# Attention steps and state-space links ahead of fill products in a list scheduler, with paired whole-float32 score products and norm sums as small products

## The chip, the cores and the metric

One core of a Trainium2 chip runs the whole program. The metric is the device time of one execution in microseconds; the kernel before was timed three times (2448.54, 2445.88 and 2444.16 us, median 2445.88). One more execution was profiled; all rows below are from it.

## The reference

The input is one sequence of 512 tokens with 1024 features. Four blocks follow each other, all in float32, each a mixer and a SwiGLU feed-forward layer, with RMS norms ahead of each:

1. a bidirectional mLSTM mixer;
2. a windowed attention: 16 query heads, 4 key heads of 64 features, blocks of 128 queries that see the block before, their own and the next one, with a learned sink;
3. a parallel mixer: an attention that keeps 128 keys per query by an index score (8 index heads of 64, top-k), next to a Mamba-2 state-space part (16 heads, chunks of 128). Ahead of it stand the final norm of the first network and the norm of the second one;
4. a short convolution mixer.

```python
# index score and selection (parallel mixer)
il = jnp.einsum('bthd,bsd->bths', iq_blk, ik) * (IDX_DIM ** -0.5)
score = jnp.einsum('bths,bth->bts', jax.nn.relu(il), iw_blk)
_, sel = lax.top_k(score, topk)
...
# both attentions
p = softmax(q @ k.T * 64 ** -0.5 + mask);  o = p @ v
...
# state-space part, per chunk
y_diag = jnp.einsum('bclsgr,bcsgrp->bclgrp', cb[..., None] * decay, xdt)
hs = hs * dec[..., None, None] + st
```

## The kernel before

The activations stay in eight tiles `xT` (128 features x 512 tokens). A weight product takes three float32r products: weight and activation are each split in a high and a low part (`whi`, `wlo`; `xh`, `xl`), and `mm3` or `mm3n` (L205 to L214) adds high x high, high x low and low x high in a PSUM bank. ScalarE makes the high part (L171) and VectorE or GpSimd the low one (L166).

The program is written once, in Python, and a list scheduler then sets the order on each engine: an instruction's place in the program is its priority, and among those whose inputs are there, by the scheduler's own clock, the earliest in the program goes first. So the order of the text decides who goes first, and PSUM banks (eight, dealt out by `share` to the tags g, s, t and o) and buffers decide when something can start.

**Norm** (`norm`, L255 to L311). Squares are summed over the eight tiles on VectorE (L272), `col_sums` (L236) makes column sums by products with ones (L239), `rsqrt_cols` (L226) runs three Newton steps on 128x4 values, and `bcast_rows` (L242) spreads the result by four transposes (L245). Ahead of the parallel mixer there are two norms one after the other: each tile is squared, scaled in place by the final norm's weight (L277), split (L279, L280) and squared again, and the second factor is worked out from the first (L291 to L298).

**Window attention** (`window`, L947). `attend(g, c, y)` (L1003) does four heads of one query block: two pairs of score products with 64 contracted rows (L1015; the two heads of a pair stand on partitions 0 to 63 and 64 to 127), mask and maximum on VectorE (L1020), exponential on ScalarE (L1023), transposes (L1027), a copy (L1030, L1032), products with the values into two halves of a bank (L1036), and a last scaling by transposed reciprocals (L1047, L1050). Between the 16 calls stand fill products: the remaining query projections with `rope`, and parts of the output product. Banks are 1, 3, 3, 1 for g, s, t, o.

**Parallel mixer** (`parallel`, L1077). `index` (L1144) makes index scores, per head with a stacked high/low query (`pair_stack`, L926) and key (`key_stack`, L932): one product over 128 rows (L943) and one over 64 (L944). `topk_rounds` (L1169) finds the 128 largest per row in 16 rounds of MAX8 and MATCH_REPLACE8 on VectorE for each of three query blocks; `pump` issues some of them between other work. `att_head` (L1374) is one head of one block: three float32r score products (L1380), mask (L1381), exponential (L1387), transposes (L1391), a split of the probabilities in high and low (L1393 on ScalarE, L1394 on VectorE) and three products with split values (L1402). `fill` issues projections for the state-space part (24 products each) between the heads. Then `group_start`, `group_block` and `group_end` (L1465, L1522, L1547) make the chunk states (transposes L1470 and L1483, state products L1492, scaling L1485 to L1497), the outputs (L1531, L1534, decays from a DMA in `decays`) and a norm, with the output product `add_out` (L323) between them.

## Time and profile before

| | |
|---|---|
| runs (median of 3) | 2445.88 us |
| profiled execution, its own time | 2444.67 us |
| its span, first to last instruction | 2442.9 us |
| around the span | 1.8 us |
| TensorE (PE) busy | 2387.8 us, 98% of the span |
| weight loads (PEld) | 2055.9 us, 84% |
| VectorE (DVE) | 1804.2 us, 74% |
| ScalarE (ACT) | 1198.3 us, 49% |
| GpSimd (POOL) | 361.2 us, 15% |
| DMA | 93 GB/s on average |
| chain of work that ended last | PE 90%, DVE 5%, DMA 2% |
| granted TensorE clock, mean | 0.99 |

An instruction's busy time on PE has a modelled end and overlaps the next one; how much PE time a product takes is therefore read from one start to the next, and the chain of waits prints just that. A whole-float32 product is recorded as two MATMULs, a float32r product as one, so "x4" of a score line in the chain is two score products. Window attention runs from about 604 to 830 us, the double norm from 1160, index scores from 1211, top-k and attention of the parallel mixer to 1411, and the state-space part to about 1530 us.

### The profile page before, as it was taken

Reading aid. Unit: us, or ns where it says so; the run is one execution under the profiler, and the core shown is the slowest. Engines: PE = TensorE matmul, PEld = TensorE weight load, DVE = VectorE, ACT = ScalarE, POOL = GpSimd, SP = SyncE. Lnnn points to the kernel's source line nnn. Section 1 sums busy time; section 2 is a strip of 40 time slices with the busy share of each in tenths; the row PEclk is TensorE's granted clock in tenths of the full one; section 3 lists DMA queues with packets and bytes.
Section 4 is the critical chain, followed back from the end, with each engine's and each line's share of the span. In section 5 each row is a group of like instructions: output and inputs, shape, how many; then the busy total and the mean of one; then the engine's idle time right before and its main releaser. Section 6 shows DMA issues by size and latency. Waiting matters only on the chain.

```text
span 2442.9 us, 36706 instructions
## 1 busy us (share of the span) xinstructions
PE 2387.8 (98%) x13956; PEld 2055.9 (84%) x13956; DVE 1804.2 (74%) x3063; ACT 1198.3 (49%) x2226; POOL 361.2 (15%) x252
## 2 busy tenths in 40 slices
PE   8999999999999999999899989999999999999998
PEld 7898899998656899999677867888989788899997
DVE  7676798777564787877789778786867755668877
ACT  4444545454464554545566564553635324445444
POOL 2210001010320001010354145100100010000100
PEclk9999999999999999999999999999999999999999
DMA  5332232323211232323222132232323323223232
GB/s 167 117 100 61 78 117 96 113 87 119 82 51 35 69 113 88 120 87 110 78 71 61 53 111 87 87 100 82 121 87 104 104 96 100 81 88 120 87 104 78
DMA packets 73440, 226.64 MB, mean 93 GB/s; under 512 B 10336, under 2 KB 14576, under 8 KB 73264
## 3 DMA queue, kind: packets, MB, share of 16 engines
q1 hardware_dynamic: 68896, 220.00, 28.0%
q10 hardware_dynamic: 4320, 4.21, 0.6%
q8 instruction: 109, 1.79, 0.3%
q14 instruction: 67, 0.55, 0.1%
q0 software_dynamic: 48, 0.10, 0.0%
HBM read 219.45 MB, written 2.20 MB: 91 GB/s over the span
## 4 chain that ended last, share of the span: by engine, by line
PE 90%; DVE 5%; DMA 2%; ACT 1%; issue 1%; POOL 0%; ACTq 0%; SPq 0%; POOLq 0%; DVEq 0%
PE ps_g L206 7%; PE ps_g L208 7%; PE ps_g L207 7%; PE ps_s L206 4%; PE ps_s L208 4%; PE ps_s L207 4%; PE ps_g L446 4%; PE ps_g L444 4%; PE ps_g L445 4%; PE ps_t L206 3%; PE ps_t L207 3%; PE ps_t L208 3%; PE ps_t L446 3%; PE ps_t L445 3%; PE ps_t L444 3%; PE ps_s L1015 2%
## 5 line engine op out<-in xcount | busy, mean ns | idle before, releaser
L171 ACT ACTIVATE whi<-wraw 128x512 fp32r<-128x512 f32 (+1 forms) x726 | 447.3, 621 | 667.7 <-PE ps_g L207 236.6
L166 DVE TENSOR_TENSOR wlo<-wraw,whi 128x512 fp32r<-128x512 f32 x666 | 490.3, 746 | 188.5 <-ACT whi L171 176.1
L206 PE MATMUL ps_g<-xh,whi 128*128 128x512 f32 (+1 forms) x696 | 279.7, 404 | 2.9 <-DVE ct L1611 2.1
L424 POOL TENSOR_TENSOR S<-wraw 128x1024 f32<-128x1024 f32 x36 | 106.9, 2971 | 1173.3 <-DMA wraw<-in_in_dram 760.3
L207 PE MATMUL ps_g<-xl,whi 128*128 128x512 f32 (+1 forms) x696 | 278.1, 400 | 0.0
L208 PE MATMUL ps_g<-xh,wlo 128*128 128x512 f32 (+1 forms) x696 | 277.8, 399 | 0.0
L171 ACT ACTIVATE whi<-S 128x512 fp32r<-128x512 f32 x288 | 178.2, 628 | 191.3 <-PE ps_g L445 58.2
L166 DVE TENSOR_TENSOR wlo<-S,whi 128x512 fp32r<-128x512 f32 x288 | 199.8, 719 | 34.8 <-ACT whi L171 32.9
L444 PE MATMUL ps_g<-thi,whi 128*128 128x256 f32 x576 | 164.1, 285 | 2.7 <-ACT whi L171 1.9
L446 PE MATMUL ps_g<-thi,wlo 128*128 128x256 f32 x576 | 164.1, 285 | 0.2
L206 PEld LDWEIGHTS ps_g<-xh,whi 128*128 128x128 f32 (+1 forms) x696 | 132.1, 190 | 37.8 <-issue 5.6
L445 PE MATMUL ps_g<-tlo,whi 128*128 128x256 f32 x576 | 163.7, 284 | 0.0
L208 PEld LDWEIGHTS ps_g<-xh,wlo 128*128 128x128 f32 (+1 forms) x696 | 132.0, 190 | 31.6 <-issue 4.4
L207 PEld LDWEIGHTS ps_g<-xl,whi 128*128 128x128 f32 (+1 forms) x696 | 132.2, 190 | 29.1 <-issue 3.5
L444 PEld LDWEIGHTS ps_g<-thi,whi 128*128 128x128 f32 x576 | 111.4, 193 | 3.3 <-ACT whi L171 2.1
L446 PEld LDWEIGHTS ps_g<-thi,wlo 128*128 128x128 f32 x576 | 111.4, 193 | 0.7 <-DVE wlo L166 0.7
L445 PEld LDWEIGHTS ps_g<-tlo,whi 128*128 128x128 f32 x576 | 111.3, 193 | 0.0
L166 POOL TENSOR_TENSOR wlo<-wraw,whi 128x512 fp32r<-128x512 f32 (+1 forms) x60 | 81.0, 1359 | 153.4 <-ACT whi L171 110.5
L207 PE MATMUL ps_s<-hlo,whi 128*128 128x512 f32 x264 | 102.8, 389 | 0.0
L208 PE MATMUL ps_s<-hhi,wlo 128*128 128x512 f32 x264 | 102.7, 389 | 0.0
L206 PE MATMUL ps_t<-hhi,whi 128*128 128x512 f32 x264 | 102.7, 389 | 0.0
L207 PE MATMUL ps_t<-hlo,whi 128*128 128x512 f32 x264 | 102.7, 389 | 0.0
(545 smaller groups left out, 6641.2 us busy)
## 6 DMA issues: line engine op xcount, KB each, us to landing
wraw<-in_in_dram SPq DMA_DIRECT2D x176, 512.0 KB, 3.5
wraw<-in_down_dram SPq DMA_DIRECT2D x82, 512.0 KB, 3.6
wraw<-in_par_in_dram SPq DMA_DIRECT2D x30, 512.0 KB, 3.3
wraw<-in_mlstm_in_dram SPq DMA_DIRECT2D x24, 512.0 KB, 3.6
wraw<-in_sc_in_dram SPq DMA_DIRECT2D x24, 512.0 KB, 3.5
wraw<-in_attn_in_dram SPq DMA_DIRECT2D x12, 512.0 KB, 3.4
wraw<-in_par_out_dram SPq DMA_DIRECT2D x12, 512.0 KB, 3.5
mb<-drs SPq DMA_DIRECT2D x16, 256.0 KB, 4.1
```

Source lines behind the costliest of these rows:

```text
L166: (V if e == "V" else G).tensor_tensor(lo, x, hi.bitcast(F32), op=ALU.subtract)
L171: A.activation(hi, raw, AF.Copy)
L206: T.matmul(o, lhsT=w[0], rhs=x[0], start=start, stop=False)
L207: T.matmul(o, lhsT=w[0], rhs=x[1], start=False, stop=False)
L208: T.matmul(o, lhsT=w[1], rhs=x[0], start=False, stop=stop)
L424: G.tensor_tensor(live[jj, "S1"], live[jj, 2], live[jj, 3], op=ALU.add)
L444: T.matmul(o, lhsT=w[0], rhs=x[i][0], start=start and i == j == 0, stop=False, skip_group_check=True)
L445: T.matmul(o, lhsT=w[0], rhs=x[i][1], start=False, stop=False, skip_group_check=True)
L446: T.matmul(o, lhsT=w[1], rhs=x[i][0], start=False, stop=end, skip_group_check=True)
L1015: T.matmul(ps[:, 0:n], lhsT=Q[2 * g + j][a, sl], rhs=K[pair][a, ks], start=True, stop=True)
```

## The change

1. `ahead_of_fills` runs a function at a priority 400 places earlier. It is put around `attend`, `att_pair`, `att_end`, `group_start`, `group_block`, `group_end`, and the sums and rows of each norm.
2. `side_by_side` issues the two score products of a pair next to each other in two banks, and makes both wait until both banks have been read (`busy`), so that no other product stands between them. `rotate` sets the order in which banks are taken. The window layer's banks become 1, 4, 2, 1.
3. Index scores, attention scores and the products with the values in the parallel mixer become whole float32 products in pairs, without split parts; heads are done two at a time (`att_pair`). The value products of a pair start with the upper half.
4. The double norm takes both sums of squares from one tile of squares by products with two columns (`pcol`: ones and squared weight), accumulated over the tiles in one bank. The tiles are no longer scaled in place; weight and factor go into `xT` in one instruction each during the attention of the last two blocks.

```diff
+    def rotate(tag, order):
+        ids = sorted(set(banks[tag][0]))
+        banks[tag] = [[ids[i] for i in order], 0]
+    def side_by_side(products, tag="s"):
+        tiles, ids = [], []
+        for _ in products:
+            names, n = banks[tag]
+            ids.append(names[n])
+            tiles.append(bank(tag))
+        with tc.high_priority(HP):
+            for f, ps in zip(products, tiles):
+                ins = f(ps)
+                for i in ids:
+                    if i in busy:
+                        tc.add_manual_dep(ins.ins, busy[i].ins.name, SYNC)
+        return list(zip(ids, tiles))
+    def ahead_of_fills(f, *args):
+        with tc.high_priority(HP):
+            return f(*args)
...
+        if pre:
+            both = bank(tag)
+            for k in range(KT):
+                sq = row_tile()
+                A.activation(sq, xT[k], AF.Square)
...
+                for c in range(NCH):
+                    T.matmul(both[:, 2 * c:2 * c + 2], lhsT=sq[:, c * P:(c + 1) * P], rhs=pcol[:, 2 * k:2 * k + 2],
+                             start=k == c == 0, stop=k == KT - 1, skip_group_check=True)
...
-        xs.sums, xs.rows = scales, rows
+        xs.sums, xs.rows = lambda: ahead_of_fills(scales), lambda: ahead_of_fills(rows)
...
-        share([1, 3, 3, 1])
+        share([1, 4, 2, 1])
+        rotate("s", (0, 1, 2, 3, 1, 0, 3, 2))
...
-                    T.matmul(ps[:, 0:n], lhsT=Q[2 * g + j][a, sl], rhs=K[pair][a, ks], start=True, stop=True)
+                pss = side_by_side([lambda ps, a=a: T.matmul(ps[:, 0:n], lhsT=Q[2 * g + j][a, sl], rhs=K[pair][a, ks],
+                                                             start=True, stop=True) for a in halves])
...
-                for r, a in enumerate(halves):
+                for r, a in ((1, halves[1]), (0, halves[0])):
...
-                attend(g, c, y)
+                ahead_of_fills(attend, g, c, y)
...
+        rotate("s", (0, 1, 0, 2))
...
-                pair_stack(r, par, q2)
-                    scores(ps[:, 0:n], q2, par, ikh, ikl, slice(c * P, (c + 1) * P), slice(0, n))
+                pss = side_by_side([lambda ps, a=a: T.matmul(ps[:, 0:n], lhsT=iq[b][a, c * P:n], rhs=ik[a, 0:n],
+                                                             start=True, stop=True) for a in halves])
...
-            for i, (x, z) in enumerate(((0, 0), (1, 0), (0, 1))):
-                T.matmul(ps[:, 0:n], lhsT=q[x][a, c * P:n], rhs=k[z][a, 0:n], start=i == 0, stop=i == 2)
+            pss = side_by_side([lambda ps, a=a: T.matmul(ps[:, 0:n], lhsT=q[a, c * P:n], rhs=k[a, 0:n],
+                                                         start=True, stop=True) for a in halves])
...
-            A.activation(hi[:, 0:n], pt[:, 0:n], AF.Copy)
-            V.tensor_tensor(lo[:, 0:n], pt[:, 0:n], hi[:, 0:n].bitcast(F32), op=ALU.subtract)
+                if par and c >= 2:
+                    V.tensor_copy(t[:, 0:n], pt[:, 0:n])
+                else:
+                    A.activation(t[:, 0:n], pt[:, 0:n], AF.Copy)
...
-                for i, (v, t) in enumerate(((vh, hi), (vh, lo), (vl, hi))):
-                    T.matmul(o[0:m, h // 2 * P:h // 2 * P + P], lhsT=v[:, 0:m], rhs=t[:, sl],
-                             start=j == 0 and i == 0, stop=j == c and i == 2)
+                for par, a in ((1, halves[1]), (0, halves[0])):
+                    T.matmul(o[a, b * P:(b + 1) * P], lhsT=va[j][:, P * b + 64 * par:P * b + 64 * par + 64],
+                             rhs=pts[par][:, sl], start=j == 0, stop=j == c)
...
-            for h in (1, 0, 3, 2, 5, 4, 7, 6):
-                att_head(c, h, o, mx, den)
+            for b in range(H // 2):
+                ahead_of_fills(att_pair, c, b, o, mx, den)
+                if after_final and c >= 2:
+                    k = 4 * (c - 2) + b
+                    with tc.issue_after(latest[0].ins):
+                        V.scalar_tensor_tensor(xT[k], xT[k], col("fin", k), xs.rb1, op0=ALU.mult, op1=ALU.mult)
...
-        g0 = group_start(0)
+        g0 = ahead_of_fills(group_start, 0)
...
-            group_block(0, g0, b, dec)
+            ahead_of_fills(group_block, 0, g0, b, dec)
```

How this moves instructions is shown at three places, all on TensorE.

The first is the window attention, where its third group of heads begins. L1015 is a score product, L1027 the transposes of probabilities, L1036 the value products, L1047 the last transposes. Before:

```order
L1015 MATMUL ps_s<-q_6625,q_6954 128x256
L1027 MATMUL ps_t<-ident,prob 128x128 x2
L1015 MATMUL ps_s<-q_6625,q_7046 128x256
L1027 MATMUL ps_t<-ident,prob 128x128 x2
L1015 MATMUL ps_s<-q_6625,q_7046 128x256
L1047 MATMUL ps_t<-ident,rdb 128x128 x2
L1027 MATMUL ps_t<-ident,prob 128x128 x2
L1015 MATMUL ps_s<-q_6625,q_6954 128x384
L1036 MATMUL ps_o<-pT,va 64x256 x4
```

And now, from the last pair of the second group on (L1064, L1077, L1086 and L1097 are the same four):

```order
L1064 MATMUL ps_s<-q_6596,q_6840 128x256 x2
L1077 MATMUL ps_t<-ident,prob 128x128 x6
L1064 MATMUL ps_s<-q_6629,q_6958 128x256 x2
L1077 MATMUL ps_t<-ident,prob 128x128 x3
L1097 MATMUL ps_t<-ident,rdb 128x128 x2
L1064 MATMUL ps_s<-q_6629,q_7050 128x256 x2
L1077 MATMUL ps_t<-ident,prob 128x128 x2
L1086 MATMUL ps_o<-pT,va 64x256 x6
L1077 MATMUL ps_t<-ident,prob 128x128 x6
L1064 MATMUL ps_s<-q_6629,q_6958 128x384 x2
```

A score product stood alone between transposes and the two of a pair apart; now each pair is one row of x2.

The second is the double norm ahead of the parallel mixer, from its last sums to the first index scores. L239 are the sums, L245 the spreading of the factor, L1124 the transposes of the index weights; L206 to L208 are projection products. Before, with 20 projection products between L239 and the first L245, and 4 between the two L245:

```order
L239 MATMUL ps_t<-ones,ssum 128x1 x4
L206 MATMUL ps_g<-xh,whi 128x512
...
L207 MATMUL ps_g<-xl,whi 128x512
L245 MATMUL ps_t<-ident,nrc 128x128 x4
L208 MATMUL ps_g<-xh,wlo 128x512
...
L208 MATMUL ps_g<-xh,wlo 128x512
L245 MATMUL ps_t<-ident,nrc 128x128 x4
L1124 MATMUL ps_t<-ident,ikw 128x8 x4
```

And now (L322 are the small products of the sums, L275 the spreading), with 32 projection products between L322 and the first L275, 10 to the second, and 33 more behind that:

```order
L322 MATMUL ps_t<-pcol,rb 128x2 x8
L236 MATMUL ps_g<-xh,whi 128x512
...
L237 MATMUL ps_g<-xl,whi 128x512
L275 MATMUL ps_t<-ident,nrc 128x128 x4
L238 MATMUL ps_g<-xh,wlo 128x512
...
L238 MATMUL ps_s<-xh,wlo 128x512
L275 MATMUL ps_t<-ident,nrc 128x128 x4
L236 MATMUL ps_g<-xh,whi 128x512
```

The sums stand earlier, more products stand behind them, and the index weights' transposes are further down.

The third is the start of the state-space part. L1470 and L1483 are transposes, L1492 a state product. Before:

```order
L1470 MATMUL ps_t<-ident,F 128x128 x4
L1483 MATMUL ps_t<-ident,N 128x128 x12
L1492 MATMUL ps_o<-xe,bn 128x512
L1483 MATMUL ps_t<-ident,N 128x128 x4
L1470 MATMUL ps_t<-ident,F 128x128 x4
L1492 MATMUL ps_o<-xe,bn 128x512
L1483 MATMUL ps_t<-ident,N 128x128 x2
L206 MATMUL ps_g<-N,whi 128x512
```

And now (L1523, L1536, L1545 are the same; L1584 are output products that stood as L1531), with 23 and 18 products of other projections in the two gaps:

```order
L1523 MATMUL ps_t<-ident,F 128x128 x4
L1536 MATMUL ps_t<-ident,N 128x128 x4
L237 MATMUL ps_g<-xl,whi 128x512
...
L238 MATMUL ps_g<-xh,wlo 128x512
L1536 MATMUL ps_t<-ident,N 128x128 x8
L1545 MATMUL ps_o<-xe,bn 128x512
L236 MATMUL ps_g<-xh,whi 128x512
...
L238 MATMUL ps_g<-N,wlo 128x512
L1536 MATMUL ps_t<-ident,N 128x128 x4
L1523 MATMUL ps_t<-ident,F 128x128 x4
L1584 MATMUL ps_s<-m,xd 64x128
L1545 MATMUL ps_o<-xe,bn 128x512
```

What stood as one chain of transposes and state products now has 41 fill products in it.

## Rows read from the trace of the kernel before

**Rows 1.** Stages: busy us of PE, PEld, DVE, ACT, POOL; PEclk, DMA share, GB/s.

```profile
700.00:720.00 20.00, 20.00 (x103) 10.72 (x103) 12.40 (x45) 13.26 (x43) 4.26 (x3) 1.00 0.14 41
1180.00:1206.00 26.00, 18.88 (x92) 15.00 (x91) 20.97 (x47) 11.66 (x20) 8.79 (x7) 0.91 0.31 98
1310.00:1350.00 40.00, 40.00 (x217) 31.67 (x216) 38.40 (x90) 29.10 (x68) 19.68 (x16) 1.00 0.17 53
```

**Rows 2.** Chain that ended last, from 642 us: start us, us until the next piece.

```profile
642.59 1.15 PE ps_s L1015 x2
...
655.50 0.84 PE ps_s L1015 x2
...
658.87 0.84 PE ps_s L1015 x4
...
666.94 0.57 PE ps_o L1036 x2
...
671.00 0.63 PE ps_s L1015 x4
...
677.86 1.45 PE ps_o L1036 x12
...
1185.30 0.79 PE ps_t L239 x8
```

**Rows 3.** Groups of TensorE instructions: busy us, mean ns | idle before them.

```profile
L1027 PE MATMUL ps_t<-ident,prob 128*128 128x128 f32 x160 | 29.5, 292 | 3.4 <-ACT prob L1023 3.4
L1036 PE MATMUL ps_o<-pT,va 128*64 128x256 f32 x160 | 27.8, 393 | 0.0
...
L1015 PE MATMUL ps_s<-q,q 64*128 64x384 f32 x64 | 25.3, 547 | 0.0
...
L1015 PE MATMUL ps_s<-q,q 64*128 64x256 f32 x64 | 19.1, 435 | 0.5 <-POOL q L974 0.5
```

**Rows 4.** TensorE in order of time, norm ahead of the parallel mixer: start us, us.

```profile
1201.01 0.84 PE L245 MATMUL ps_t<-ident,nrc 128*128 128x128 f32 x4 [4.61 <-DVE nrc L298]
1204.03 0.57 PE L1124 MATMUL ps_t<-ident,ikw 8*128 8x8 f32 x4 [2.18 <-DVE ikw L1120]
...
1205.97 0.63 PE L206 MATMUL ps_g<-xh,whi 128*128 128x512 f32 x1
1206.40 0.63 PE L207 MATMUL ps_g<-xl,whi 128*128 128x512 f32 x1
```

**Rows 5.** The same view, index scores of one head.

```profile
1237.28 0.28 PE L943 MATMUL ps_s<-ikh,q 128*128 128x256 f32 x1
...
1238.54 0.50 PE L208 MATMUL ps_g<-xh,wlo 128*128 128x512 f32 x1
...
1241.17 0.39 PE L943 MATMUL ps_s<-ikh,q 128*128 128x512 f32 x1
...
1241.91 0.50 PE L207 MATMUL ps_g<-xl,whi 128*128 128x512 f32 x1
```

**Rows 6.** Chain that ended last, attention of the parallel mixer.

```profile
1345.87 0.72 PE ps_s L1380 x3
...
1350.97 0.89 PE ps_s L1380 x3
...
1387.69 1.90 PE ps_o L1402 x23
```

**Rows 7.** Busy time of L1176, then of L1177 alone, 1259 to 1366 us.

```profile
1259.00:1366.00 107.00, 26.45 (x48) 0.98 0.22 69
...
1259.00:1366.00 107.00, 28.69 (x94) 0.98 0.22 69
```

**Rows 8.** TensorE waits, 1405 to 1515 us: total us, times, longest.

```profile
PE ps_g L206 <- DVE xT L338: 5.5, 3, 4.6
PE ps_t L1483 <- DVE xd L1485: 2.2, 1, 2.2
```

**Rows 9.** VectorE in order of time, state-space part.

```profile
1457.10 0.69 DVE L1539 TENSOR_TENSOR N<-N,F 128x512 f32<-128x512 f32 x1 [5.34 <-POOL N L1538]
```

More of the change, by code (lines that the diff above doesn't have):

```diff
@@ L261, in norm @@
         xs.t = []
-        sums = [scr("ssum", bufs=1)]
-        if pre:
-            sums.insert(0, row_tile())
+        sums = [None, None] if pre else [scr("ssum", bufs=1)]
         def square(k, ssum):
@@ L287, in scales @@
                 v = scr("nv", (P, NCH))
-                V.tensor_scalar(v, col_sums(ssum, tag), 1.0 / D, None if i else EPS, op0=ALU.mult,
+                total = col_sums(ssum, tag) if ssum else both[:, i:2 * NCH:2]
+                V.tensor_scalar(v, total, 1.0 / D, None if i else EPS, op0=ALU.mult,
                                 **({} if i else dict(op1=ALU.add)))
@@ L304, in rows @@
                 xs.rb1 = bcast_rows(rcs[0], row_tile(), tag)
-        xs.sums, xs.rows = scales, rows
+        xs.sums, xs.rows = lambda: ahead_of_fills(scales), lambda: ahead_of_fills(rows)
         if not later:
-            scales()
-            rows()
+            xs.sums()
+            xs.rows()
         return xs
@@ L1280, in parallel @@
             ps = group_a(xs, [cb[i]], ["g"])[0]
+            if i == 0:
+                index_weights()
             index(i)
@@ L1453, in parallel @@
         wo = "par_out"
-        if after_final:
-            for k in range(KT):
-                V.tensor_tensor(xT[k], xT[k], xs.rb1, op=ALU.mult)
         class group:
```

143 lines of the change are left out of this document (73 added, 70 removed).

## The prediction, made before the changed kernel ran

> **What bounds the kernel now.** The page comes first: TensorE (PE) is busy for 98% of the span and carries 90% of the chain that ended last. Busy is not peak, so I went on to the table by stage, to see whether another engine sets the pace where the change works. In the window layer PE is busy for all of 20 us, ScalarE for 13.3 and VectorE for 12.4 [rows 1]: PE is the bound there, and what PE spends on attention is the time of the layer. In the double norm PE is busy for 18.9 of 26 us at a granted clock of 0.91, and VectorE for 21: the norm's chain is the bound. From 1310 to 1350 us PE is full, but VectorE has 38.4 of 40 us too, half of it top-k: MAX8 and MATCH_REPLACE8 take 26.5 and 28.7 us between 1259 and 1366 us [rows 1, 7]. There both must get shorter for the stage to get shorter. Then I read how long single products hold PE, in the chain of waits, from one start to the next. A 384-column score alone holds it 0.84 us (x2, one product); two next to each other hold it 0.84 us as well (x4), and two of 256 columns 0.63 [rows 2]. So whenever a pair is torn apart, its second score is paid in full.
>
> **The change part by part**, all against the profiled execution's 2444.7 us.
>
> *Window scores.* The 64 products hold PE 25.3 + 19.1 = 44.4 us [rows 3]. As 32 pairs they would take 16 x 0.84 + 16 x 0.63 = 23.5, which is 20.9 less. Of this some 3.9 us stay: the first chain waits 3.4 us for an exponential when there is nothing else to do [rows 3], and its score runs at the lower clock, 1.15 us [rows 2]. That leaves 17. I take 13, because ScalarE is already busy two thirds of the time in the densest part, and transposes lose a bank (3 to 2), so part of the freed time becomes waiting. Ends: 0 and 20.9. The new wait for both banks of a pair holds up the fill products behind it on PE, for one exponential at most; with four banks the pair's banks were last used two pairs ago, so I cost it at nothing.
>
> *Window value products.* Groups of three pairs take 1.45 us, but the lower half alone costs 0.57 first [rows 2]. They hold 27.8 us [rows 3]. Each of 16 calls starting as pairs gives 8 x 1.45 + 8 x 1.02 = 19.8 (1.02 is 1.45 less one pair of 0.43, the step between three and two). Less 8.0; I take 6, as not every call was torn. Ends 0 and 8.
>
> *Double norm.* Added: 32 small products at 0.79 / 4 = 0.20 us, less two old groups of 0.79 [rows 2]: +4.7 us on PE. Removed: 14 additions and 8 scalings from VectorE, 8 squares from ScalarE. More important, both sums are there two tiles earlier, and 42 products (32 small ones and 10 fills) stand between them and the second spreading, where 24 stood. The small ones cover 32 x 0.20 = 6.4 us, the fills 10 x 0.215 = 2.1 (half of the 0.43 us at which they step at half the clock, below), which is more than the 4.6 us waited now. So the waits of 4.6 and 2.2 us [rows 4] should go (6.8 us), and the clock need not fall: behind them products stand 0.43 us apart, start to start, and run 0.63 us [rows 4], the lower of the two levels (1.2 GHz), which I put at 2 us lost. Together 4.7 - 6.8 - 2, so -4. Ends +4.7 (the waits stay) and -4.
>
> *Index scores.* One head takes 1.26 us for two blocks and 0.74 for the third [rows 5], so eight take 16.0. Twelve pairs take 4 x (0.63 + 0.84 + 1.05) = 10.1; 1.05 for 512 columns is an estimate, the step of 0.21 from 256 to 384 taken once more. -6. The 16 stacking instructions on VectorE and ScalarE go too.
>
> *Attention scores of the parallel mixer.* Three products take 0.89 us for 512 columns, 0.72 for 384 [rows 6], by the same step 0.55 and 0.38: 8 x 2.54 = 20.3, of which about 2 overlapped already. As pairs: 4 x (0.42 + 0.63 + 0.84 + 1.05) = 11.8. -6.
>
> *Its value products.* 24 products of two heads take 1.90 us and a little [rows 6], 0.08 each; 240 take 19. As 40 whole pairs of 128 columns, half of the window's 0.43: 8.6, plus 0.15 to start each of 16 groups: 11. -8. Waits for the low part on VectorE go as well; I count none.
> On VectorE 32 subtractions go from this part, and 8 copies and 8 instructions on `xT` come; top-k stays. The two get shorter together, so I let PE's saving stand.
>
> *State-space part.* Fill products now stand in the chain of transposes and state products, so the 2.2 us wait of L1483 should go, and with it others of its kind. But the largest, 5.5 us of L206 for L338 [rows 8], comes from VectorE, which stood 5.3 us in front of L1539 for GpSimd [rows 9] while the only g bank waited to be read behind it. Putting the group's steps further forward does not remove that. I take -8; ends +8 (one more such wait and a little) and -18.
>
> *Nothing elsewhere.* Up to the window layer and in the feed-forward layers PE's products are the same in number. DMA moves 93 GB/s and the loads are unchanged.
>
> Sum: 13 + 6 + 4 + 6 + 6 + 8 + 8 = 51. 2444.7 - 51 = 2393.7; the median of the runs is 1.2 above the profiled execution, so **2395 us**.
>
> **The rivals.**
> *More is freed.* Window scores give 17, the value products 8, the state-space part 18: 16 more, 2379 us. For it: PE is full in nearly every stage. Against: the waits of [rows 8, 9] start on other engines.
> *Half comes back.* The attention chains run into ScalarE, the two transpose banks and top-k: the window scores give nothing, index and value products of the first three blocks nothing more than VectorE allows (8 back), the state-space part 3: 13 + 8 + 5 = 26 back, 2421 us. For it: VectorE with 38.4 of 40 us [rows 1].
> *It does not pair.* If two scores do not run at once, the change does not do what it says. A whole product of 384 columns takes 0.84 us alone against 0.72 for three split ones [rows 2, 6]. Then the window's scores take twice 23.5, 47 us, and with the 3.9 of waiting 6.5 more than the 44.4 of now, where I forecast 13 less: 19.5 back. The index scores take 20 instead of 10 and the attention's 24 instead of 12: 10 and 12 back. Together 42, 2437 us. Against: the x4 rows. The Trainium skill, "FP8 and Floating Point Precision", section "TensorE Precision Notes", says that a true float32 product makes four passes through the array, where the split takes three single ones; 0.84 against 0.72 agrees with the direction.
> *Slower.* A step in front reaches the head of PE's queue before its releaser is done, and the fills that used to cover it stand behind it. The price is that of a chain with nothing in front of it: 3.4 us, seen once [rows 3]. There are 16 calls in the window layer and 16 pairs in the parallel mixer. It decides from 51 / 3.4 = 15 exposed chains on; with 24 of the 32 it is 24 x 3.4 = 82 us: 2395 + 82 = 2477 us. For it: the order comes from the scheduler's own clock, not the chip's. Against: the 160 transposes of the kernel before waited 3.4 us in all [rows 3].
>
> **How the numbers follow.** Forecast 0.58, with a range of its own of 2379 to 2410; more 0.13; half back 0.18; not paired 0.03; slower 0.08. The range 2370 to 2427 holds the forecast, most of the two next to it, and the ends of the state-space part. Measurements of this kernel tell 0.2% (5 us) from no change: faster takes the first four cases (0.92) less their upper tails, 0.89; the same 0.03; slower 0.08.
>
> **What would show it.** In the chain of waits of the changed kernel score rows of x4 at 0.84 and 0.63 us should stand almost everywhere, and score groups of the window hold about 27 us in place of 44.4. Rows of L275 should have no wait of over 1 us in front. Index, attention and value products of the parallel mixer should hold about 33 us. The stretch of top-k should be some 8 us shorter. The prediction is wrong if PE's waits in the window layer sum to over 10 us, if pairs take over 1.2 us, or if the state-space part is not shorter.

## The result, and the profile after

The changed kernel takes 2410.30 us (median of 4 executions, 2407.93 to 2413.92) where the kernel before, on the same chip, takes 2445.02 us: a ratio of 0.9857 (95% interval 0.9845 to 0.9870), 34.7 us less. Timed again for the experiments it took 2409.35 us against 2448.57, ratio 0.9843 (0.9830 to 0.9856). The forecast was 2395 us, the range 2370 to 2427: the sign and the range held, but 51 us were promised and two thirds of them came. 2410.30 us lies just outside the forecast's own range (2379 to 2410), and nearer to the rival "half comes back" (2421) than to 2395.

To see where, I laid the traces over each other at products that both kernels have in the same order, and took the time from one such product to the next. The second column of the changed kernel is its second trace.

| stretch, by the trace of before | changed, first trace | changed, second | place in front gone | pairs gone |
|---|---|---|---|---|
| 0 to 630 us, same order in both | +2.8 | -1.4 | +0.8 | +0.3 |
| window layer, 630 to 855 us | -14.5 | -16.1 | -18.6 | +0.5 |
| first Strassen products behind it, 855 to 891 us | +5.0 | +5.3 | +5.3 | +5.7 |
| 891 to 1166 us, same order | 0.0 | 0.0 | 0.0 | 0.0 |
| 1166 us to the end (double norm, parallel mixer, the rest) | -24.4 | -24.6 | -21.8 | -10.0 |
| sum | -31.0 | -36.9 | -34.2 | -3.4 |

The first row is nothing that the change does: the order there is that of before. Over the thirteen traces of the change and the experiments that stretch came out between 1.4 us shorter and 3.9 us longer than in the trace of before, and most of the difference is there within the first 20 us, where TensorE waits for the input (the 51st product starts at 17.5 us before, at 20.9 and 17.4 us in these two traces). Without it the two traces of the changed kernel stand at -33.9 and -35.5.

The stretches that answer to [rows 1], of the changed kernel's first trace (us, then busy time and instructions of PE, PEld, VectorE, ScalarE, GpSimd, then granted clock, DMA share, GB/s); the second one is the double norm, the third top-k beside attention, the last the first Strassen products behind the window layer:

```profile
696.00:716.00 20.00, 17.70 (x111) 9.59 (x109) 12.62 (x44) 13.78 (x46) 4.37 (x3) 1.00 0.14 40
1166.00:1192.00 26.00, 26.00 (x143) 22.06 (x143) 8.92 (x36) 10.81 (x19) 9.29 (x8) 1.00 0.22 65
1295.00:1335.00 40.00, 40.00 (x228) 29.32 (x228) 39.66 (x93) 31.71 (x71) 22.56 (x17) 1.00 0.21 67
843.00:884.00 41.00, 36.93 (x265) 35.18 (x264) 40.14 (x51) 23.65 (x37) 5.71 (x2) 0.92 0.26 90
```

The double norm, 18.9 us busy in 26 at a clock of 0.91 before, is now full at 1.00. Top-k's stretch is as full on VectorE (39.7 of 40) as it was. New is the last row: VectorE has 40.1 of 41 us, TensorE 36.9, and the clock falls to 0.92. In the kernel before the same products ran in 36.2 us at the full clock, with VectorE just as full:

```profile
854.85:891.00 36.15, 35.09 (x267) 33.49 (x266) 36.15 (x47) 21.41 (x34) 2.75 (x1) 1.00 0.31 103
```

The groups of the window layer (busy us, mean ns | idle before them), as [rows 3] has them:

```profile
L1077 PE MATMUL ps_t<-ident,prob 128*128 128x128 f32 x160 | 30.0, 289 | 5.1 <-ACT prob L1073 3.4 <-ACT pT L1082 1.6
L1086 PE MATMUL ps_o<-pT,va 128*64 128x256 f32 x160 | 24.9, 392 | 1.5 <-DVE pT L1080 1.5
L1064 PE MATMUL ps_s<-q,q 64*128 64x384 f32 x64 | 15.4, 559 | 0.5 <-ACT prob L1073 0.3
L1064 PE MATMUL ps_s<-q,q 64*128 64x256 f32 x64 | 11.9, 428 | 0.6 <-POOL q L1023 0.4 <-ACT prob L1073 0.2
```

Busy times overlap, so I summed what the products hold, from each one's start to the start of the next product. Scores: 28.5 us, of which 3.5 is the wait for the first exponential (43.6 before by the same sum). Value products: 24.5, of which 1.4 is a wait (26.0 before). Transposes: 23.9 (22.5 before).

The chain that ended last, in the parallel mixer (start us, us, what):

```profile
1304.01 0.84 PE ps_s L1429 x4
...
1328.97 0.81 PE ps_o L1454 x12
...
1335.83 1.06 PE ps_s L1429 x4
```

A score pair (x4) of 384 columns holds 0.84 us, one of 512 columns 1.06 us, and six pairs of value products (x12) 0.81 us. All 16 pairs of attention scores stand whole, and 31 of the 32 of the window layer.

The norm's spreading, in order of time (TensorE; a bracket behind a row would be a wait), as [rows 4]:

```profile
1186.02 0.39 PE L237 MATMUL ps_g<-xl,whi 128*128 128x512 f32 x1
1186.25 0.60 PE L275 MATMUL ps_t<-ident,nrc 128*128 128x128 f32 x4
...
1188.98 0.60 PE L275 MATMUL ps_t<-ident,nrc 128*128 128x128 f32 x4
...
1189.65 0.39 PE L237 MATMUL ps_g<-xl,whi 128*128 128x512 f32 x1
```

No wait stands ahead of L275, and the products behind it are 0.23 us apart. But at the end of the index scores there is a new wait (all engines between two score products, some rows left out):

```profile
1250.61 1.13 PE L1208 MATMUL ps_s<-ik,iq 64*128 64x512 f32 x4
...
1251.77 1.08 ACT L1213 ACTIVATE rel<-ps_s 128x512 f32<-128x512 f32 x2 [0.52 <-PE ps_s L1208]
...
1252.40 1.83 DVE L1217 SCALAR_TENSOR_TENSOR sc<-rel,iw,sc 128x512 f32<-128x512 f32 x1
1252.42 1.26 POOL L196 TENSOR_TENSOR wlo<-wraw,whi 128x512 fp32r<-128x512 f32 x1
...
1254.55 0.74 DVE L1217 SCALAR_TENSOR_TENSOR sc<-rel,iw,sc 128x512 f32<-128x512 f32 x1
...
1255.54 0.67 DVE L1330 TENSOR_TENSOR kh<-ps_g,ssum 128x512 f32<-128x512 f32 x1
...
1256.31 0.80 PE L1429 MATMUL ps_s<-kh,N 64*128 64x128 f32 x4 [4.58 <-issue]
...
1257.63 0.63 PE L237 MATMUL ps_g<-cy,whi 128*128 128x512 f32 x1
```

TensorE makes the last pair of index scores (L1208) and has nothing until the first attention score (L1429) at 1256.31. ("Issue" means that the profile shows no releaser; the rows in between do.) ScalarE evacuates the index scores, VectorE adds them up (L1217, twice), and only then reaches the keys (L1330) that the attention score reads. Behind the wait the products stand 0.43 us apart, start to start (1257.63 and the next at 1258.06), at the lower of the two clock levels.

TensorE's waits in the state-space part (total us, times, longest), as [rows 8]:

```profile
PE ps_o L1587 <- DVE pv L1552: 2.8, 1, 2.8
PE ps_s L1584 <- DVE m L1578: 2.0, 2, 1.5
PE ps_o L1545 <- ACT pv L1548: 1.8, 1, 1.8
...
PE ps_s L1584 <- POOL m L1578: 0.5, 1, 0.5
...
PE ps_o L1545 <- DVE pv L1552: 0.4, 1, 0.4
```

The 5.5 us of the evacuation behind L1539 are gone; what is left are mostly waits of links of the chain itself.

For the stretch from 1166 to 1582 us before, 1159 to 1548 after, the same sum (each product's start to the next one's, waits and clock included) gives all of TensorE's time by kind of product:

| products | before, us | after, us | difference |
|---|---|---|---|
| attention scores | 18.1 | 12.5 | -5.6 |
| attention values | 22.7 | 12.3 | -10.4 |
| index scores | 15.6 | 16.0 | +0.5 |
| column sums, small products with `pcol` among them | 4.9 | 10.2 | +5.3 |
| spreading of norms | 4.8 | 2.8 | -2.0 |
| fills with `xh`, `xl` (941 and 942) | 237.0 | 229.3 | -7.7 |
| products with `cy` (48), behind the index scores | 11.6 | 14.6 | +3.0 |
| state-space transposes and products | 38.5 | 31.4 | -7.2 |
| output products with `N` (192) | 50.5 | 47.0 | -3.5 |
| all else | 12.4 | 13.3 | +0.9 |
| sum | 416.0 | 389.3 | -26.7 |

### The profile page after: what moved, and what is told of

It is laid out like the page before. It is cut to its first block, busy times and chain, and to the rows that moved or that the text cites. A ratio compares the mean times of both kernels' runs of the same rounds, so it can differ in the third digit from the quotient of the medians.

```text
span 2412.2 us, 36473 instructions
## 1 busy us (share of the span) xinstructions
PE 2354.2 (98%) x13892; PEld 2030.9 (84%) x13892; DVE 1762.4 (73%) x2995; ACT 1182.2 (49%) x2194; POOL 350.4 (15%) x251
## 5 line engine op out<-in xcount | busy, mean ns | idle before, releaser
L196 DVE TENSOR_TENSOR wlo<-wraw,whi 128x512 fp32r<-128x512 f32 x666 | 491.9, 749 | 196.3 <-ACT whi L201 167.9
L236 PE MATMUL ps_g<-xh,whi 128*128 128x512 f32 (+1 forms) x696 | 279.3, 402 | 3.4 <-DVE ct L1664 2.1
L196 DVE TENSOR_TENSOR wlo<-S,whi 128x512 fp32r<-128x512 f32 x288 | 199.9, 720 | 34.4 <-ACT whi L201 32.5
L493 PE MATMUL ps_g<-thi,whi 128*128 128x256 f32 x576 | 164.2, 285 | 2.2 <-ACT whi L201 1.4
L236 PEld LDWEIGHTS ps_g<-xh,whi 128*128 128x128 f32 (+1 forms) x696 | 131.8, 189 | 33.9 <-issue 3.6
L493 PEld LDWEIGHTS ps_g<-thi,whi 128*128 128x128 f32 x576 | 111.3, 193 | 3.1 <-ACT whi L201 1.9
L236 PE MATMUL ps_t<-hhi,whi 128*128 128x512 f32 x264 | 102.7, 389 | 0.0
L238 PE MATMUL ps_t<-hhi,wlo 128*128 128x512 f32 x264 | 102.7, 389 | 0.0
```

Of the source, the lines that this page charges most:

```text
L196: (V if e == "V" else G).tensor_tensor(lo, x, hi.bitcast(F32), op=ALU.subtract)
L236: T.matmul(o, lhsT=w[0], rhs=x[0], start=start, stop=False)
L238: T.matmul(o, lhsT=w[1], rhs=x[0], start=False, stop=stop)
L493: T.matmul(o, lhsT=w[0], rhs=x[i][0], start=start and i == j == 0, stop=False, skip_group_check=True)
```

## The experiments

All twelve were timed in five rounds beside the kernel before on the same chip. In short, with the ratio to the kernel before and its 95% interval:

| kernel | us | ratio |
|---|---|---|
| the change, two measurements | 2410.30, 2409.35 | 0.9857 (0.9845 to 0.9870), 0.9843 (0.9830 to 0.9856) |
| nothing put in front | 2411.27 | 0.9845 (0.9831 to 0.9858) |
| pairs torn | 2440.86 | 0.9966 (0.9953 to 0.9978) |
| window layer alone | 2435.31 | 0.9945 (0.9933 to 0.9958) |
| double norm of before | 2414.48 | 0.9875 (0.9862 to 0.9889) |
| first Strassen sum on VectorE | 2411.16 | 0.9864 (0.9848 to 0.9880) |
| window layer not in front | 2405.75 | 0.9842 (0.9829 to 0.9855) |
| first query block not in front | 2411.60 | 0.9868 (0.9855 to 0.9881) |
| last index pair behind the keys | 2409.98 | 0.9859 (0.9844 to 0.9873) |
| the same, window not in front | 2407.96 | 0.9849 (0.9834 to 0.9864) |
| state-space part not in front | 2419.41 | 0.9896 (0.9880 to 0.9913) |
| xT scaled late | 2412.61 | 0.9872 (0.9857 to 0.9886) |

The medians stand beside different chips (2444.0 to 2448.6 for the kernel before); the ratios are what can be compared. 0.001 of a ratio is 2.4 us.

### The change once more

No edit.

> The changed kernel once more, as the mark for its variants on the same chip: 2410 us, 2405 to 2415. In its first trace the first 630 us, whose order is that of the kernel before, were 2.8 us longer than there; if that belongs to one execution and not to the change, the same stretch comes out within 1 us of the kernel before now.

2409.35 us, as expected. The first 630 us were 1.4 us shorter than in the kernel before, not within 1 us, but on the other side from the first trace: that stretch belongs to the execution.

### Is it the place in front, or the pairs?

```diff
     def ahead_of_fills(f, *args):
-        with tc.high_priority(HP):
-            return f(*args)
+        return f(*args)
...
-        with tc.high_priority(HP):
-            for f, ps in zip(products, tiles):
-                ins = f(ps)
+        for f, ps in zip(products, tiles):
+            ins = f(ps)
```

> No step is put forward any more (attention steps, pairs, state-space links and norm sums keep their place in the text); whole float32 products, pairs with their common wait and the small norm products stay. Theory A, the gain comes from products that hold TensorE for less time: at most 8 us of the 35 go, 2410 to 2418 us, and the score pairs stay whole. Rival B, putting forward is what counts, because the chains then start early enough: more than half of the 35 goes, 2428 us or more.

```diff
-        with tc.high_priority(HP):
-            for f, ps in zip(products, tiles):
-                ins = f(ps)
-                for i in ids:
-                    if i in busy:
-                        tc.add_manual_dep(ins.ins, busy[i].ins.name, SYNC)
+        for f, ps in zip(products, tiles):
+            f(ps)
```

> The pairs lose their common wait and their own place in front, so that fill products come between the two halves; everything else stays. Theory A: a torn pair pays its second score in full. 32 window pairs, 12 index pairs and 16 attention pairs hold 23.5 + 10.1 + 11.8 = 45 us as pairs and up to twice that when all are torn; most are torn by the order, so 25 to 40 us are lost: 2435 to 2450 us, the window's scores near 44 us again. Rival B: the fills that come between do the same work elsewhere, less than 10 us lost, under 2420.

Theory A held twice. With nothing put in front the kernel keeps the whole gain, 2411.27 us (0.9845, in both intervals of the change, at the edge of the first): the common wait alone keeps 57 of the 60 pairs whole. With the pairs torn 2440.86 us remain, 31.5 more than the change on the same chip, where the change gains 39.2. This edit takes away the common wait and the pair's own place in front at once; whether that place would keep the pairs whole without the wait was not run. In that trace the window's scores hold 46.2 us instead of 28.5, the index scores 20.6 instead of 16.0, the attention scores 18.3 instead of 12.5, from start to start: 28.1 of the 31.5. Of the 32 window pairs 7 are still whole. One torn pair and one that happened to stay whole, in the chain of waits of that kernel (L1060 is the score's line there; x4 a pair, x2 one product):

```profile
651.74 0.84 PE ps_s L1060 x2
...
653.41 0.84 PE ps_s L1060 x2
...
655.38 0.84 PE ps_s L1060 x4
```

0.84 us for one product, 0.84 us for two.

### The window layer alone

```diff
 kernel before
+        share([1, 4, 2, 1])
+        rotate("s", (0, 1, 2, 3, 1, 0, 3, 2))
...
+                pss = side_by_side([...])
...
+                for r, a in ((1, halves[1]), (0, halves[0])):
...
+                ahead_of_fills(attend, g, c, y)
```

> The kernel before with the change of the window layer alone (attention steps in front, pairs, banks 1, 4, 2, 1, upper half of the value products first). Theory: 14 us less at the end of the window layer as in the trace of the changed kernel, of which the first Strassen products of the feed-forward layer behind it give 5 back, since they wait for VectorE: 9 us less, 2436 us (2433 to 2439). Rival: the 5 us were one execution's, and 14 remain, 2431; or the window gives nothing without the rest, 2445.

2435.31 us, in the theory's range, but on a chip where the kernel before takes 3.6 us more: the gain of 13.3 us lies between the theory's 9 and the rival's 14. In its trace the window layer is 16.6 us shorter (842 us at its end against 855, with 3.9 us lost ahead of it), the Strassen products behind it give 6.1 back, and from 1166 us on, where only the scheduler's order changed a little, it is another 2.9 shorter. So the giving back is real and is there without the rest of the change. The net is 4 us better than expected: 2.9 from those products on, and 2.1 more in the window layer than in the trace that the expectation went by (14.5), less 1.1 more given back. The same order of that layer took between 13.0 and 16.6 us off in eight traces.

### The double norm

```diff
 changed kernel, norm(), with pre
-            both = bank(tag)
...
-                    T.matmul(both[:, 2 * c:2 * c + 2], lhsT=sq[...], rhs=pcol[:, 2 * k:2 * k + 2], ...)
+                square(k, sums[0])
+                V.tensor_scalar(xT[k], xT[k], col(pre, k), None, op0=ALU.mult)
...
+            square(k, sums[-1])
```

> The changed kernel with the double norm of the kernel before: squares summed on VectorE, tiles scaled in place, column sums by products with one column; all else stays, the place of the norm's sums in front included. Theory: what stopped the waits ahead of the parallel mixer is the sums by small products, not their place. The waits of 4.8 and 2.5 us behind the spreading come back with a few smaller ones and the lower clock, 9.4 us by the sums of TensorE's waits, and 4.7 us of small products go: 5 us slower than the changed kernel, 2414 to 2415. Rival: the place in front alone does it, then 4.7 us of work go and no wait comes: 2405.

2414.48 us. Its ratio is 0.0018 and 0.0032 above the two of the change (4 and 8 us; its interval overlaps the first of the change's two and just misses the second), and its trace is 6.9 us longer from 1166 us on (-17.6 against -24.4 and -24.6). The waits are back (total us, times, longest), with the place in front kept:

```profile
PE ps_t L275 <- DVE nrc L329: 3.1, 1, 3.1
PE ps_g L236 <- DVE ikw L1153: 2.1, 1, 2.1
```

With the small waits they sum to 8.6 us from start to start, against 9.9 before the change and 0.6 after it. So it is the sums that come early, not the place in front. The trace without any place in front says the same: no wait stands ahead of its spreading. The clock was 0.87 from 1170 to 1196 us.

### The 5 us behind the window layer

```diff
-                G.tensor_tensor(live[jj, "S1"], live[jj, 2], live[jj, 3], op=ALU.add)
+                (V if jj == 2 else G).tensor_tensor(live[jj, "S1"], live[jj, 2], live[jj, 3], op=ALU.add)
```

(In the feed-forward layers blocks 0 and 1 are done plainly, so block 2 is the first Strassen one.)

> The changed kernel, but the first sum of weights for the Strassen products of each feed-forward layer is made on VectorE (about 1.2 us) in place of GpSimd (2.7 us). Beside the GpSimd instruction the step L449 took 2.52 us in the trace, 0.42 elsewhere, and behind it the window layer's gain shrank by 5.3 us. Theory: that collision is what gives the 5 us back; VectorE saves 2.1 and pays 1.2, twice or three times in the program, and the first products wait less: 2 to 5 us faster, 2405 to 2408. Rival: VectorE's chain is the bound there whatever GpSimd does, and gets 1.2 us longer: 2410 to 2413.

What started it, in the first trace of the changed kernel (VectorE and GpSimd in order of time):

```profile
842.62 0.42 DVE L450 TENSOR_TENSOR fu<-S,fu 128x256 f32<-128x256 f32 x1
...
842.96 0.69 DVE L447 TENSOR_TENSOR fu<-S 128x512 f32<-128x512 f32 x1
...
843.17 2.73 POOL L473 TENSOR_TENSOR S<-wraw 128x1024 f32<-128x1024 f32 x1 [80.01 <-DVE fu L450]
...
843.68 2.52 DVE L449 TENSOR_TENSOR fu<-S,fu 128x256 f32<-128x256 f32 x1
```

L449, 0.41 to 0.43 us in 13 of its 16 places, takes 2.52 us here, and ends 0.3 us after GpSimd does. With the sum on VectorE it takes 0.42 us, as thought; but TensorE's waits stay (that kernel, 836 to 860 us):

```profile
PE ps_g L493 <- ACT whi L201: 2.7, 1, 2.7
PE ps_g L495 <- DVE wlo L196: 1.5, 1, 1.5
PE ps_t L495 <- DVE wlo L196: 0.7, 1, 0.7
```

4.9 us, against 4.0 by the same view of the changed kernel (2.1 for `whi`, 1.4 for `wlo`, 0.5), and the time is 2411.16 us. The time is not told apart from the change; by the waits the rival held: VectorE has no idle time to give there (40.1 of 41 us), and a step that it does sooner is followed by 1.2 us more of its own. The kernel before had the same collision (L400, 2.51 us at 849.45) and waited 1.1 us in all at these products. What differs is the order on TensorE. L245 and L275 spread the norm's factor, L444 and L493 are the first Strassen products. Before:

```profile
837.23 0.60 PE L245 MATMUL ps_t<-ident,nrc 128*128 128x128 f32 x4
...
851.97 0.28 PE L444 MATMUL ps_g<-xh,whi 128*128 128x256 f32 x1
```

And in the changed kernel:

```profile
830.13 0.60 PE L275 MATMUL ps_t<-ident,nrc 128*128 128x128 f32 x4
...
840.35 0.28 PE L493 MATMUL ps_g<-xh,whi 128*128 128x256 f32 x1
```

63 projection products stood in between, 14.4 us; now 43 do, 9.9 us, in this trace and in those of all the experiments. The other 20 stand earlier. So TensorE comes to the Strassen products 4.5 us sooner after the spreading, and VectorE's work for them starts with that factor. It is not the shorter window layer that brings the waits: with the pairs torn that layer gained nothing, TensorE came to these products 0.9 us later than before, and 5.7 us were lost there all the same. That the missing cover is the cause is argued from these traces; no run changed this order alone.

### The window layer not in front

```diff
-                ahead_of_fills(attend, g, c, y)
+                attend(g, c, y)
```

and the pairs of this layer with their common wait but without a place in front.

> The changed kernel with the window layer's attention steps and pairs no longer put forward; pairs, their common wait and the banks stay, the rest keeps its place in front. In the trace without any place in front the window layer was 2.4 us shorter and the parallel mixer 2.8 us longer. Theory: putting forward costs in the window layer, because it tears the value products (10 of 25 groups with a single pair; without it only groups of two and three): 2 to 3 us faster than the changed kernel, 2407 to 2408. Rival: the 2.4 us were chance of one execution: 2410.

2405.75 us, the least of all, but its ratio of 0.9842 is that of the change (0.9843): not told apart. What the edit does to the order is clear: value products stand in 16 whole groups of two or three pairs and hold 21.0 us, as they do where nothing is put in front, instead of 25 groups and 24.5 us. 1.3 of the 21.0 is a wait; the rest, 19.7, is the 19.8 that I had forecast for whole groups. Putting the steps in front is what tore them. What it does to the layer is less clear: 18.6 us less than before in this trace and in the one with nothing in front, 16.0 in the trace of the combination below, and between 13.0 and 16.1 in seven traces that have the change's own order there.

### The wait ahead of the first attention score

```diff
-                ahead_of_fills(att_pair, c, b, o, mx, den)
+                (ahead_of_fills if c else lambda f, *x: f(*x))(att_pair, c, b, o, mx, den)
```

and the same for the pair's own place.

> The changed kernel, but the four pairs of the first query block in the parallel mixer are not put forward, so that some fill products come ahead of them. Theory: the wait of 4.6 us ahead of the first attention score is one of a step put forward whose input (the keys, behind index sums on VectorE) isn't there yet; six fill products ahead take about 1.3 us of it: 1 to 3 us faster, 2407 to 2409. Rival: the wait is there without any place in front too (4.2 us in that trace, on a fill product), VectorE's line is the cause and nothing changes: 2410.

2411.60 us: nothing gained. The wait is as long, and now stands ahead of the fill product that came in front (L236 `ps_g<-cy`, TensorE in order of time):

```profile
1249.71 1.13 PE L1208 MATMUL ps_s<-ik,iq 64*128 64x512 f32 x4
1255.37 0.80 PE L236 MATMUL ps_g<-cy,whi 128*128 128x512 f32 x1 [4.53 <-DVE kh L1330]
```

The fill waits for a bank that the keys' evacuation (L1330) frees. So it is not a step put too far in front; VectorE is late. Nor is it that the index scores became shorter: with the pairs torn they hold 15.7 us without the wait, as much as before the change, and the wait ahead of the first attention score is 4.9 us. Before the change 30 projection products stood between the last index score and the first attention score, from 1259.33 to 1266.39 us; in the changed kernel and in the one with torn pairs none does. The next run changes VectorE's line instead:

```diff
             index(2 + i)
...
+            if len(qk["k"]) == 1:
+                index(3, [NCH - 1])
```

with the last pair (`c = 3`) taken out of the loop.

> The changed kernel, but the last pair of index scores is issued behind the first key evacuation instead of ahead of it, so that on VectorE the keys no longer stand behind the two sums of that pair. Theory: TensorE's wait of 4.6 us ahead of the first attention score comes from VectorE's line (a sum that waits for ScalarE, then 1.83 us beside GpSimd and 0.74 us, then the keys); the wait falls to 1 to 2 us and the kernel gains about 3: 2406 us where the changed kernel has 2409. Rival: VectorE has no time to spare in this stretch, the wait only moves to the next product that needs a bank: no change.

> The last pair of index scores behind the first keys, and the window layer's attention steps not put forward, together. If both gains hold and add up (2 to 3 us each by the traces), 4 to 6 us faster than the changed kernel, about 2404 us; if both were chance, 2409.

The wait went down as expected, to 1.9 us, and another came (1240 to 1400 us of that kernel):

```profile
PE ps_o L1547 <- ACT pv L1550: 4.0, 1, 4.0
PE ps_s L1431 <- ACT rel L1213: 1.9, 1, 1.9
```

A state product, L1547, now waits 4.0 us for ScalarE, and the kernel takes 2409.98 us: the rival's "the wait only moves", though to a place 140 us further on. TensorE's waits in the stretch sum to 8.2 us, against 8.3 and 7.1 in the change's two traces; that the one wait brought the other is not shown. The two edits together gave 2407.96 us, ratio 0.9849: not told apart from the change either. No version beats the change beyond the interval.

### The state-space part

```diff
-        g0 = ahead_of_fills(group_start, 0)
+        g0 = group_start(0)
...
-            ahead_of_fills(group_block, 0, g0, b, dec)
+            group_block(0, g0, b, dec)
```

and so for all eight places of `group_start`, `group_block` and `group_end`.

> The changed kernel without putting the state-space steps forward (start, blocks and end of both groups). TensorE's waits between the attention and the feed-forward layer sum to 27.5 us before the change, 15.8 and 17.5 in two traces after it, 20.1 where nothing is put forward. Theory: the place in front is worth 3 to 4 us of these and the rest comes from elsewhere (the xT instructions that moved out of this stage): 2412 to 2413 us. Rival: the place in front carries the 10 to 12 us: 2419 us or more.

```diff
                 ahead_of_fills(att_pair, c, b, o, mx, den)
-                if after_final and c >= 2:
-                    k = 4 * (c - 2) + b
-                    with tc.issue_after(latest[0].ins):
-                        V.scalar_tensor_tensor(xT[k], xT[k], col("fin", k), xs.rb1, op0=ALU.mult, op1=ALU.mult)
...
         wo = "par_out"
+        if after_final:
+            for k in range(KT):
+                V.scalar_tensor_tensor(xT[k], xT[k], col("fin", k), xs.rb1, op0=ALU.mult, op1=ALU.mult)
```

> The changed kernel, but the eight instructions that scale xT stand again at the start of the state-space part, where the kernel before has its own eight, instead of beside the attention. Theory: VectorE then starts that stage some 6 us late, and evacuations that TensorE's only g bank waits for come behind them as before: waits of the stage 5 to 8 us longer than in the changed kernel's 15.8 to 17.5, 2414 to 2417 us. Rival: VectorE has time there and the attention gets shorter by as much: 2409.

Without its place in front the state-space part costs 2419.41 us, 0.0039 and 0.0053 of a ratio above the change (9.5 and 13 us): the rival's time came. Its waits, 1379 to 1490 us, are links and evacuations in equal parts:

```profile
PE ps_o L1545 <- POOL xe L1542: 2.9, 1, 2.9
PE ps_t L269 <- POOL ssum L1598: 2.8, 1, 2.8
PE ps_o L1545 <- ACT pv L1548: 2.8, 1, 2.8
PE ps_g L236 <- DVE xT L387: 2.6, 2, 1.5
```

From start to start all waits of the stage sum to 23.7 us, 6 to 8 more than with the change. (These sums take from each step what is more than its kind of product usually holds, the slower clock included; by the view above alone the waits are 14.5 us, as before the change, and 8.4 in both traces with it.) From 1166 us on the trace is 7.5 us longer than those of the change, which these waits account for; the rest lies in the window layer and behind it, whose order is the same. But it does not fit with the first pair of experiments: where nothing is put in front, attention included, the stage waits 20.1 us and the whole loses nothing that can be measured. So the place in front of the state-space steps is worth these 7 to 13 us only as long as other steps have one. Attention steps in front leave more fill products for later, which then stand in front of links that have no place; this is how I read it, and no run tried attention alone at other distances.

With `xT` scaled late the kernel takes 2412.61 us, 0.0015 and 0.0029 above the change (4 and 7 us; its interval overlaps the first of the change's and just misses the second), and its trace is 2.8 us longer from 1166 us on than the mean of the change's two. The waits of the stage are 20.6 us against 15.8 and 17.5: the theory's direction, at half its size.

## Why the prediction was right, and where it was not

**What bounds the kernel** was read rightly: TensorE is full, what it holds counts, and a torn pair pays its second score in full. Tearing the pairs alone loses 31.5 of the 39.2 us that the change gains on that chip. That two products on two halves take the time of one held for every size: 0.63, 0.84 and 1.06 us (1.05 had been estimated for 512 columns). The rival "it does not pair" is out, and "slower" with it: the exposed chain it spoke of came once, not 15 times.

**Window scores**, forecast -13: 43.6 to 28.5 us, -15. Right. The wait of 3.4 us stayed, as the sum had it. TensorE's waits in the layer sum to 8.7 us, under the 10 that would have shown the prediction wrong.

**Window value products**, forecast -6: 26.0 to 24.5, -1.5. This step failed, for two reasons. The 27.8 us that it started from are busy time, which overlaps; from start to start the products held 26.0, so that 1.8 of the gain was never there. And its 19.8 us supposed that every call starts with whole pairs; the upper half now comes first, but with the steps in front the products go out one pair at a time as transposed probabilities arrive, ten times of 25. Without the place in front they are whole and hold 21.0.

**Double norm**, forecast -4: the old norm in the changed kernel costs 4 and 8 us by the ratios, 6.9 by the traces. Right, and rather too small: the small products cost 5.3 us in place of 4.7, but small waits that the two rows of the sum did not have go too (9.9 us in all, against the 6.8 counted). The reason given holds: the cover is the sums' early arrival. But the cover was misread: the 42 products between the last small ones and the second spreading are all projection products (32 and 10), where 24 stood; the small ones stand ahead of them and cover nothing. With the first spreading among them they take 10.2 us, from 1178.81 to 1188.98.

**Index scores**, forecast -6: the pairs hold 10.2 us, as was worked out (10.1), when the waits behind them are taken off. But 4.6 us of TensorE's time is lost at the end of the stage and 1.2 earlier, so that they take 16.0 as before (15.6), and the products with `cy` behind the wait pay 3.0 more, at the lower clock. The step that failed is that the sum counted no wait here, although VectorE works on the results: index sums and keys stand in one line there, and the 30 products that covered this line on TensorE stand elsewhere now. The wait is there with torn pairs too, so it is the order that opened it and not the saving. With it the index, attention and value products hold 40.8 us together, where the prediction's sign was 33.

**Attention**, scores -6 and value products -8: 18.1 to 12.5 and 22.7 to 12.3 us, -16 together. Right, a little more, and all of that in the value products: they held 22.7 us where the sum had started from 19. VectorE was as full as before beside top-k, and the stage from the first score to the last value product went from 144 to 124 us, more than the 8 us I had named for the stretch of top-k: that VectorE must get shorter too had been true for 40 us of it, not for the whole.

**State-space part**, forecast -8 with ends of +8 and -18: the state-space products and the output products between them hold 10.7 us less, and TensorE's waits went from 27.5 to 15.8 and 17.5 us. (The waits are part of what the products hold; the two don't add up.) The mechanism was partly the one given: links put in front cost 7 to 13 us when they alone lose their place, but hardly anything when every step does. The eight `xT` instructions that left this stage carry some of it (4 and 7 us by the ratios of the run that put them back), which I had counted nowhere, and the wait of 5.5 us that I thought would stay is gone.

**Nothing elsewhere** failed: the Strassen products behind the window layer lose 5 us. The products there are the same in number, as the prediction says, but not in order: 20 fewer stand between the norm's factor and the Strassen products that VectorE prepares. The rival "half comes back" had put such a loss down to shorter attention chains, the transpose banks and top-k; this one comes without a shorter window layer too.

The account, by the first trace: the window layer took 14.5 off where 19 had been forecast, the products behind it gave 5 back, the norm and the parallel mixer took 26.9 off instead of 32 (the index scores with the clock behind them 9 to 10 short, the rest 4 to 5 better), and the last 800 us, whose order hardly changed, were 2.5 us longer (not longer in the second trace, so that term belongs to the execution). 51 - 4.5 - 5 - 5 - 2.5 = 34, which is what the trace shows without its first 630 us.

**The place in front**, which the change has in its first words, is worth nothing measurable as a whole (0.9845 without it). The prediction had not separated it from the pairs.

The Trainium skill, "FP8 and Floating Point Precision", section "TensorE Precision Notes", has four passes for a true float32 product. The rows bear on it only by ratio: 0.84 us for one whole product or two at once, against 0.72 for three split ones of one head; whole products pay only when they stand in pairs, and torn they lost nearly the whole gain.

## What to carry to other kernels

Before you reorder for a bound engine, look for two instructions that can share it and ask what holds them together: here pairs kept whole were worth 31 us, a common wait on both banks was enough to keep them so, and the place in the queue was worth nothing that could be measured. For each place where the order changes, write down which other engine prepares the next inputs, and count the products that stand between the start of its chain and the first one that needs it; behind the window layer 20 fewer stood there, behind the index scores 30 fewer, and about 5 us were lost at each. And try a place in front for parts of a chain with care: in one of the three kernels that took it from a part alone, the state-space steps, this cost 7 to 13 us, in the other two nothing.

## What was not expected of the hardware

**VectorE beside GpSimd.** L449 takes 0.42 us, and 2.52 us when it starts 0.51 us after a GpSimd instruction of 2.73 us; it ends 0.30 us after that one's end. L1217 takes 0.74 us, and 1.83 us beside L196 on GpSimd, which started 0.02 us later. The Trainium skill, "SBUF — State Buffer", section "Who interferes with whom", says that a VectorE instruction with two inputs in SBUF contends with a GpSimd instruction that reads SBUF, for ports that only one of them holds at a time, and that the order of issue decides which one waits. The first pair of rows agrees. In the second VectorE started first by the trace's times and was held up all the same, so with starts this close the order in the trace did not tell who waits.

**Executions of one order differ.** The first 630 us, the same instructions in the same order, differ by 5.3 us between traces, most of it from the first 20 us. The window layer with one order took 13.0 to 16.1 us less than before in seven traces, and its granted clock from 680 to 730 us was 1.00 in some and 0.97 in others. Differences of 3 us between two single traces are therefore no evidence. I had built two expectations on them (the window layer not in front, alone and combined), and neither kernel stands apart from the change.

**The clock behind a wait.** After the 4.6 us ahead of the first attention score fill products stood 0.43 us apart, as in [rows 4], where a wait of the same length was; ahead of it they stood 0.23 us apart.
